# Linear ReLU attention: every octet's Q loaded between K and V, and one octet's Q in five transfers

## The chip, the cores and the metric

The kernel runs on one core of a Trainium2 chip. The metric is the device time of one execution in microseconds (us), taken as the median of several runs of the same program.

## The reference

Q, K and V are 8 x 12 heads of 512 rows of 64 numbers in fp32, the result has the same shape.

```python
Q_feat = np.maximum(0, Q)
K_feat = np.maximum(0, K)
KV = np.einsum('bhkd,bhkv->bhdv', K_feat, V)
K_sum = np.sum(K_feat, axis=2)
numerator = np.einsum('bhqd,bhdv->bhqv', Q_feat, KV)
denominator = np.einsum('bhqd,bhd->bhq', Q_feat, K_sum)
return (numerator / (denominator[:, :, :, None] + 1e-10)).astype(np.float32)
```

Nothing is quadratic in the sequence length: per head there is one 64 x 64 product of K and V, and one product of Q with it.

## The kernel before

The 96 heads are worked on as NO = 12 octets of eight heads. One octet of one tensor is 1 MB of fp32 in DRAM, seen as 128 rows (one for each partition) of 2048 numbers, 8 KB a row. The program moves 36 such blocks in and 12 out.

**Loads.** K and V of octet 0 come by SyncE (SP) in fp32 into two of the output buffers (L267). All else is loaded by GpSimd (POOL) in transfers that cast fp32 to bf16, so that a row of 8 KB arrives as 4 KB: `load_q` (L174) and `load` (L179). There are nine input buffers of each kind (`NI`), so octets 1 to 9 are issued ahead of all work, in program order, and octets 10 and 11 follow the stores of octets 0 and 1. In `load(o)` the order is K, V, Q; for the last octet alone it is K, Q, V (L182 to L187).

**Six lanes.** Each GpSimd transfer signals one of six semaphores in turn (`lane("pool")`, L163). The helper `op` (L58) lists the lane among the things that the transfer writes (L65), so a transfer waits until the one six places before it has landed. Hence six GpSimd transfers at most are in flight, and GpSimd issues the next when the oldest lands.

**One octet's work, `step(i)` (L313).** TensorE transposes Q (L360), multiplies K by V over 64 row blocks into `ps_kv` (L369), transposes the previous octet's result (L378), then computes denominators and numerators (L354). ScalarE applies relu to the transposed Q (`relu_q`, L209), evacuates K-by-V (`evac_kv`, L217), masks a quarter of the next octet's V (`prep_v` as "a0", L200) and copies the numerators out (`copy_ot`, L225). VectorE copies the next octet's Q from its input buffer (`copy_q`, L206), applies relu to the next K (`prep_k`, L191), scales the previous octet's result into an output buffer (`norm`, L242), computes the reciprocals (L230, L234, L237) and masks the rest of the next V (L202). Each engine runs its own list in program order; semaphores tie them together. On ScalarE "a0" stands between `evac_kv` and `copy_ot`, on VectorE `copy_q` stands ahead of `prep_k` and `norm`.

**Stores.** There are seven output buffers (`NOUT`). The stores of octets 0 and 1 are issued by GpSimd among the loads. Those of octets 2 to 11 are issued by SP, and `store` (L246) lists the last octet's K buffer among the things that they read:

```python
keys.append(("k", (NO - 1) % NI))
do.op("sp", lambda e: e.dma_start(out=to, in_=src), reads=keys,
```

So no SP store is issued before K of octet 11 has landed. `norm(9)` writes the buffer that store 2 reads from, and so on: from there a result waits for an older store to land.

## The time and the profile before

| what | value |
|---|---|
| median of 3 runs | 125.52 us (125.49 to 125.57) |
| the profiled execution's own time | 125.56 us |
| its span on the core | 123.7 us |
| TensorE busy | 85.0 us, 69% of the span |
| VectorE busy | 82.4 us, 67% |
| ScalarE busy | 78.3 us, 63% |
| GpSimd busy | 27.6 us, 22%, in 55 instructions |
| read from and written to DRAM | 37.75 MB and 12.58 MB |
| DRAM traffic over the span | 407 GB/s |
| GpSimd transfer of 512 KB (bf16), issue to landing | median 14.4 to 14.5 us |

The span runs from the first to the last recorded event; the profiled time is 1.86 us more. The DMA row of the page is the share of time in which the 16 DMA engines have a packet, averaged over them, in 40 slices of 3.1 us. The GB/s row counts what is written, so a load that casts to bf16 shows half of what it reads.

### The profile page before, as it was taken

The page shows a single profiled execution, that of the slowest core. Times are in us where ns is not written, and L with a number is a line of the kernel's source. Part 1 is how long each engine was busy: PE and PEld are TensorE (multiplying, and loading weights), DVE is VectorE, ACT ScalarE, POOL GpSimd, SP SyncE. Part 2 cuts the span into 40 slices and gives each one's busy share as a digit, 9 for nine tenths or more (in the row PEclk, how much of TensorE's full clock was granted, in tenths as well). Part 3 has the DMA queues.
Part 4 walks back from the last instruction along what each step waited for, and adds up shares of the span by engine and source line. Part 5 has one row for each costly group of instructions (what it writes and reads, how often), then busy time and mean ns, then how long its engine had stood idle before and what let it go on. Part 6 is the DMA issues. An engine that isn't in the chain of part 4 may idle for free.

```text
span 123.7 us, 3402 instructions
## 1 busy us (share of the span) xinstructions
PE 85.0 (69%) x1440; PEld 73.5 (59%) x1440; DVE 82.4 (67%) x127; ACT 78.3 (63%) x108; POOL 27.6 (22%) x55
## 2 busy tenths in 40 slices
PE   0000097697896979969799697996978918983900
PEld 0000096686794867949589485794856916972900
DVE  1261904769789697895987959869688649067330
ACT  0000762998987889878898788987869736652000
POOL 5795311331131213312421142221000000000000
PEclk9999999999999999999999999999999996897555
DMA  3999999999999999999999999999999999999955
GB/s 69 404 315 222 213 215 212 212 212 212 216 215 215 212 212 212 217 215 213 213 215 212 212 212 267 334 215 234 354 217 212 404 424 432 421 421 429 434 238 212
DMA packets 6916, 32.55 MB, mean 263 GB/s; under 512 B 768, under 2 KB 768, under 8 KB 5120
## 3 DMA queue, kind: packets, MB, share of 16 engines
q0 software_dynamic: 5184, 19.93, 75.8%
q1 hardware_dynamic: 1728, 12.58, 24.7%
q14 instruction: 3, 0.02, 0.0%
q8 instruction: 1, 0.02, 0.0%
HBM read 37.75 MB, written 12.58 MB: 407 GB/s over the span
## 4 chain that ended last, share of the span: by engine, by line
DMA 71%; PE 8%; DVE 7%; issue 5%; POOL 4%; POOLq 0%; DVEq 0%; SPq 0%
DMA k_sb<-in_K_dram 54%; DMA q_sb<-in_Q_dram 12%; DMA out_dram<-o_sb 6%; DVE o_sb L242 5%; PE ps_x L378 4%; PE ps_kv L369 2%; POOL vo L263 2%; PE ps_qt L360 1%; DVE ot_sb L225 1%; PE ps_x L354 1%; POOL k_sb L184 1%; POOL mask L263 1%; POOL q_sb L175 1%; POOL v_sb L184 0%; DVE den L234 0%
## 5 line engine op out<-in xcount | busy, mean ns | idle before, releaser
L242 DVE TENSOR_TENSOR o_sb<-ps_x,rec 128x1024 f32<-128x1024 f32 x24 | 28.5, 1217 | 9.2 <-PE ps_x L378 6.6
L225 ACT COPY ot_sb<-ps_x 128x1024 f32<-128x1024 f32 x23 | 23.2, 1013 | 10.7 <-PE ps_x L354 9.8
L369 PE MATMUL ps_kv<-vo,kf 64*128 64x132 bf16 x768 | 26.7, 228 | 0.8 <-DVE vo L202 0.2
L378 PE MATMUL ps_x<-ident,ot_sb 128*128 128x128 f32 x192 | 25.3, 288 | 1.7 <-DVE ot_sb L225 1.7
L369 PEld LDWEIGHTS ps_kv<-vo,kf 64*128 64x128 bf16 x768 | 24.7, 99 | 2.6 <-issue 2.6
L360 PE MATMUL ps_qt<-ident,q 128*128 128x128 bf16 x192 | 14.4, 235 | 16.4 <-DVE q L206 15.4
L209 ACT ACTIVATE qt<-ps_qt 128x1024 bf16<-128x1024 bf16 x24 | 23.4, 1031 | 1.9 <-PE ps_qt L360 1.9
L378 PEld LDWEIGHTS ps_x<-ident,ot_sb 128*128 128x128 f32 x192 | 22.3, 148 | 3.2 <-issue 2.0
L360 PEld LDWEIGHTS ps_qt<-ident,q 128*128 128x128 bf16 x192 | 12.4, 106 | 19.0 <-DVE q L206 15.4
L217 ACT CAST kvd<-ps_kv 64x260 bf16<-64x260 f32 x48 | 17.9, 374 | 8.5 <-PE ps_kv L369 7.6
L354 PE MATMUL ps_x<-qt,kvd 128*128 128x256 bf16 x96 | 14.9, 281 | 12.1 <-DVE o_sb L242 12.0
L191 DVE TENSOR_SCALAR kf<-k_sb,mask 128x2048 bf16<-128x2048 bf16 x22 | 15.6, 750 | 8.5 <-PE ps_kv L369 8.4
L354 PEld LDWEIGHTS ps_x<-qt,kvd 128*128 128x128 bf16 x96 | 7.7, 100 | 16.9 <-DVE o_sb L242 16.3
L206 DVE COPY q<-q_sb 128x2048 bf16<-128x2048 bf16 x12 | 8.2, 686 | 8.6 <-DMA q_sb<-in_Q_dram 8.6
L175 POOL DMA_DIRECT2D q_sb<-in_Q_dram x12 | 9.2, 763 | 19.0 <-DMA q_sb<-in_Q_dram 14.6
L200 ACT ACTIVATE vo<-v_sb,mask 128x1024 bf16<-128x1024 bf16 x11 | 12.7, 1153 | 0.6 <-DMA v_sb<-in_V_dram 0.4
L202 DVE TENSOR_SCALAR vo<-v_sb,mask 128x2048 bf16<-128x2048 bf16 (+1 forms) x22 | 11.6, 568 | 0.0
L184 POOL DMA_DIRECT2D k_sb<-in_K_dram x11 | 7.7, 697 | 16.8 <-DMA k_sb<-in_K_dram 12.9
L184 POOL DMA_DIRECT2D v_sb<-in_V_dram x11 | 6.3, 576 | 16.5 <-DMA v_sb<-in_V_dram 12.7
L200 ACT ACT_TABLE_LOAD x1 | 1.3, 1283 | 12.2 <-DMA o_sb<-in_V_dram 12.2
L354 PE MATMUL ps_kv<-kvd,qt 128*128 128x16 bf16 x192 | 6.9, 179 | 1.7 <-ACT kvd L217 1.7
L354 PEld LDWEIGHTS ps_kv<-kvd,qt 128*128 128x128 bf16 x192 | 6.4, 96 | 2.0 <-ACT kvd L217 1.9
(21 smaller groups left out, 27.6 us busy)
## 6 DMA issues: line engine op xcount, KB each, us to landing
out_dram<-o_sb SPq DMA_DIRECT2D x10, 1024.0 KB, 12.4
q_sb<-in_Q_dram POOLq DMA_DIRECT2D x12, 512.0 KB, 14.5
k_sb<-in_K_dram POOLq DMA_DIRECT2D x11, 512.0 KB, 14.4
v_sb<-in_V_dram POOLq DMA_DIRECT2D x11, 512.0 KB, 14.4
out_dram<-o_sb POOLq DMA_DIRECT2D x2, 1024.0 KB, 14.7
o_sb<-in_K_dram SPq DMA_DIRECT2D x1, 1024.0 KB, 6.2
o_sb<-in_V_dram SPq DMA_DIRECT2D x1, 1024.0 KB, 10.7
```

What stands on the lines that cost most here:

```text
L184: do.op("pool", lambda e: e.dma_start(out=t[i], in_=X[o], single_packet=True), writes=[(n.lower(), i)], dma=lane("pool"))
L191: do.op("dve", lambda e: e.tensor_scalar(kf[:, :, s, :], src, scalar1=0.0, scalar2=mask[:, 0, s:s + 1], op0=Alu.max, op1=Alu.mult), reads= ...
L200: make = lambda e: e.activation(to, src, Act.Copy, scale=m)
L202: make = lambda e: e.tensor_scalar(to, src, scalar1=m, scalar2=None, op0=Alu.mult)
L209: do.op("act", lambda e: e.activation(qt[:, j * (U // 2):(j + 1) * (U // 2)], ps_qt[j], Act.Relu), reads=[("pq", j)], writes=[("qt", j)])
L217: do.op("act", lambda e: e.copy(kvd[64 * c:64 * c + 64, s:8:2, c * D1:c * D1 + D1].rearrange("p (g t) d -> p g t d", t=2), ps_kv[64 * s:64 ...
L225: do.op(who, lambda e: e.copy(to, src) if who == "act" else e.tensor_copy(to, src), reads=[("x", j)], writes=[("ot", j)], sem=f"t{j}")
L242: do.op("dve", lambda e: e.tensor_tensor(o_sb[i][:, rs], ps_x[j].rearrange("p (r d) -> p r d", d=D), rec[:, rs].unsqueeze(2).to_broadcast( ...
L354: return pe.matmul(out_, lhsT, rhs, start=True, stop=True, skip_group_check=True)
L360: x = pe.transpose(ps_qt[u // 8][:, u % 8, :], q2[:, u, :], ident)
L369: x = pe.matmul(ps_kv[:, h, 0:2 * (D + 2)].rearrange("p (t d) -> p t d", t=2), kf[ps, R * g + k, :, :].rearrange("p s d -> p (s d)"), vo[p ...
L378: x = pe.transpose(ps_x[u // 8][:, u % 8 * P:u % 8 * P + P], ot[:, u].rearrange("p h c -> p (h c)"), ident32)
```

## The change

Three things change in the program. `load` puts Q between K and V for every octet, as it was for the last one alone. Q of octet 6, the seventh, is issued as five transfers of 40, 11, 45, 7 and 25 rows, back to back by GpSimd; all five signal one semaphore of their own, "arc", and take no lane, so that V of octet 6 takes the lane that this Q had. Consumers wait for all five (80 counts). The Q buffers are declared flat, which leaves `copy_q` the same 2048 numbers in each partition.

```diff
+    ARCS_AT = 6
+    ARCS = (40, 11, 45, 7, 25)
...
-    def op(self, who, make, reads=(), writes=(), sem=None, dma=None, kept=False):
+    def op(self, who, make, reads=(), writes=(), sem=None, dma=None, kept=False, more=False):
...
-        if kept:
+        if kept or more:
             made.then_inc(self.sems[dma], 16)
             self.count[dma] = self.count.get(dma, 0) + 16
...
     def load_q(o):
-        do.op("pool", lambda e: e.dma_start(out=q_sb[o % NI].rearrange("p u f -> p (u f)"), in_=Qr[o],
-                                            single_packet=True),
+        if o == ARCS_AT:
+            p = 0
+            for n in ARCS:
+                rows = slice(p, p + n)
+                p += n
+                do.op("pool", lambda e: e.dma_start(out=q_sb[o % NI][rows], in_=Qr[o][rows], single_packet=True),
+                      writes=[("q", o % NI)], dma="arc", more=p < P)
+            return
+        do.op("pool", lambda e: e.dma_start(out=q_sb[o % NI], in_=Qr[o], single_packet=True),
               writes=[("q", o % NI)], dma=lane("pool"))
 
     def load(o):
         i = o % NI
         for n, X, t in (("K", Kr, k_sb), ("V", Vr, v_sb)):
-            if n == "V" and o == NO - 1:
+            if n == "V":
                 load_q(o)
             do.op("pool", lambda e: e.dma_start(out=t[i], in_=X[o], single_packet=True), writes=[(n.lower(), i)],
                   dma=lane("pool"))
-        if o < NO - 1:
-            load_q(o)
```

More of the change, by code (lines that the diff above doesn't have):

```diff
@@ L148 @@
     rec = sb.tile([P, RQ], fp32, name="rec")
-    q_sb = [sb.tile([P, U, P], bf16, name=f"q_sb{i}") for i in range(NI)]
+    q_sb = [sb.tile([P, RQ * D], bf16, name=f"q_sb{i}") for i in range(NI)]
     k_sb = [sb.tile([P, RQ * D], bf16, name=f"k_sb{i}") for i in range(NI)]
@@ L158 @@
     names = ["dve", "act", "pool", "pe", "q2", "a0", "d0", "d1", "ev", "t0", "t1", "n0", "n1"]
-    lanes = {"pool": [f"gl{i}" for i in range(LANES)], "sp": [f"sl{i}" for i in range(3)], "last": ["el"]}
+    lanes = {"pool": [f"gl{i}" for i in range(LANES)], "sp": [f"sl{i}" for i in range(3)], "last": ["el"],
+             "arc": ["arc"]}
     sems = {n: tc.alloc_semaphore("s_" + n) for n in names + sum(lanes.values(), [])}
@@ L205, in copy_q @@
     def copy_q(o):
-        do.op("dve", lambda e: e.tensor_copy(q2, q_sb[o % NI]), reads=[("q", o % NI)], writes=["q2"], sem="q2")
+        do.op("dve", lambda e: e.tensor_copy(q2.rearrange("p u f -> p (u f)"), q_sb[o % NI]), reads=[("q", o % NI)],
+              writes=["q2"], sem="q2")
     def relu_q(j):
@@ L287, in body @@
             step(o)
-        for n in lanes["pool"] + lanes["sp"]:
+        for n in lanes["pool"] + lanes["arc"] + lanes["sp"]:
             nc.gpsimd.wait_ge(sems[n], do.count[n])
```

## The prediction, made before the changed kernel ran

> **What bounds the kernel now.** I read the page's slices and its DMA queues first.

> ```profile
> DMA  3999999999999999999999999999999999999955
> ...
> q0 software_dynamic: 5184, 19.93, 75.8%
> q1 hardware_dynamic: 1728, 12.58, 24.7%
> q14 instruction: 3, 0.02, 0.0%
> q8 instruction: 1, 0.02, 0.0%
> ```

> The DMA engines are never idle between the second slice and the last two; no compute engine is above 69%. The 5184 GpSimd packets are 36 transfers x 16 engines x (8 rows + 1 completion). Besides data, four instruction packets share the engines. Next, GpSimd's timeline gives the price of a transfer.

> ```profile
> 36.62 0.53 POOL L184 DMA_DIRECT2D k_sb<-in_K_dram  x1 [1.80 <-DMA k_sb<-in_K_dram]
> 39.08 0.53 POOL L184 DMA_DIRECT2D v_sb<-in_V_dram  x1 [1.93 <-DMA v_sb<-in_V_dram]
> 41.59 0.62 POOL L175 DMA_DIRECT2D q_sb<-in_Q_dram  x1 [1.98 <-DMA q_sb<-in_Q_dram]
> ```

> Each issue waits for the transfer six back. K of octet 3 is issued at 14.54 us and K of octet 9 at 58.74, 18 transfers later: (58.74 - 14.54) / 18 = 2.456 us per 1 MB, so 2.456 / 8 = 0.307 us per row on each engine. Then the chain that ended last, near its end:

> ```profile
> 78.40 14.85 DMA k_sb<-in_K_dram
> 93.25 0.02 issue
> 93.27 7.43 DMA out_dram<-o_sb
> 100.70 0.02 issue
> 100.72 2.37 DVE o_sb L242 x2
> ...
> 117.68 1.23 DVE o_sb L242
> ```

> K of octet 11 lands at 93.25, which lets SP issue store 2; store 2 lands at 100.70, which frees the buffer for `norm(9)`; from there 23.0 us of work follow. VectorE's timeline shows how tight that is:

> ```profile
> 97.19 1.42 DVE L191 TENSOR_SCALAR kf<-k_sb,mask 128x2048 bf16<-128x2048 bf16 x2 [0.72 <-PE ps_kv L369]
> 100.72 2.35 DVE L242 TENSOR_TENSOR o_sb<-ps_x,rec 128x1024 f32<-128x1024 f32 x2 [2.11 <-DMA out_dram<-o_sb]
> ```

> VectorE sat 2.11 us for the store: this is the slack up to which an earlier landing brings the end forward one for one.

> A transfer lands when the last of its 16 engines has finished, and the trace records all 16 completions. In us from the span's start, sorted by time (not by engine number, which it doesn't give):

> ```
> transfer        1st   12th   13th   14th   15th   16th
> K, octet 2    20.16  20.39  20.45  20.53  20.56  21.64
> K, octet 11   91.48  91.83  92.01  92.12  92.16  93.25
> store 2       98.84  99.20  99.49  99.53  99.67 100.70
> store 5      106.21 106.58 106.84 106.91 107.36 108.02
> store 10     118.46 119.02 119.10 119.15 120.18 120.32
> store 11     122.57 122.70 122.72 122.73 122.74 122.75
> ```

> One engine is about 1.1 us behind the next from the start, and every wait for a transfer is a wait for it. The packet records show why: the one "q8 instruction" packet, 16 KB, starts at 4.77 us and takes 0.94 us on one engine, whose own packet beside it takes 0.81 instead of 0.31. Nothing gives the time back, since all engines then do equal work at equal speed. A second engine falls behind late (15th column, 0.1 us ahead of the 16th at store 10), after an instruction packet at 107.21 and a row of its packets at 0.35 to 0.40 us. So the bound is one engine's queue, and at the very end two engines'.

> **The change, part by part.**

> *Q ahead of V.* V of an octet now lands where Q did, one transfer later than its own former place. Its first user is ScalarE's "a0". Octet 2: Q had landed by 26.60 us, "a0" starts at 29.01; these are the rows:

> ```profile
> 26.60 0.69 DVE L206 COPY q<-q_sb 128x2048 bf16<-128x2048 bf16 x1 [1.12 <-DMA q_sb<-in_Q_dram]
> ```

> ```profile
> 29.01 1.15 ACT L200 ACTIVATE vo<-v_sb,mask 128x1024 bf16<-128x1024 bf16 x1
> ```

> That leaves 2.4 us; octets 3, 4, 5 and 10 by the same rows 2.6, 2.9, 2.9 and 2.2. If this cover went, "a0" would hold `copy_ot` behind it on ScalarE, and TensorE's L378. Q comes 2.46 us earlier, which ends VectorE's waits for it (8.6 us in 7); but the next gates, the 0.37 us of `norm(8)` for store 1 and the 2.11 us of `norm(9)` for store 2, are DMA landings. Cost and gain 0 at the end; below zero only if the waits for stores vanished, which they don't.

> *Four more issues.* An issue on GpSimd takes 0.53 to 1.52 us, so five take 2.6 to 7.6 us, from about 37.2 to 39.8 or 44.8. Behind them V of octet 6 waits, and every later load, but six transfers in flight are 6 x 2.456 = 14.7 us of work, to about 51. Cost 0. Without that cover it would be the delay past Q's old slot at 41.59, up to 3.2 us.

> *Four more completions on each engine.* Their records take 0.009 to 0.022 us, while a row follows the one before the completion after 0.306 + 0.006. 4 x 0.006 to 4 x 0.022 = 0.02 to 0.09 us; I take 0.03, by the spacing.

> The five smaller transfers themselves: the queue is full, and the nearest row is the 2.456 us spacing, 427 GB/s. [...]

> *The dealing of rows.* The trace only shows 128 rows dealt 8 to an engine. Of other counts it shows nothing: an engine may get none or several times 8, which moves its queue by -8 x 0.307 = -2.46 us or by more than that upwards. [...] The light places gain 3 x 0.307 = 0.92 and 2 x 0.307 = 0.61 us, the heavy ones lose 0.31. [...]

> *Sum.* If the light places are the two late engines: K 11 lands at 93.25 - 0.92 + 0.03 = 92.36, or, if the next engine is a heavy one, at 92.16 + 0.31 + 0.03 = 92.50. Store 2: 99.81, or 99.67 + 0.34 = 100.01. Gain at `norm(9)` 0.69 to 0.89, well inside 2.11. All later work moves along. At the end store 11 must not queue behind store 10. By the packet records it starts at 119.77 on the first engine and at 119.95 on the late one, which is busy until then; the second late one is free at 119.68. Now these two are free at 119.95 - 0.89 = 119.06 and 119.68 - 0.58 = 119.10, and store 11's issue allows 119.77 - 0.69 to 0.89 = 118.9 to 119.1: the last start moves from 119.95 to about 119.1. Net 0.8 (0.65 to 0.9). The span becomes 123.7 - 0.8 = 122.9, with the 1.86 us around it 124.76; the median is 0.04 below the profiled run: 124.72.

> **The rivals.**

> *The deal misses the late engines.* If the late engine gets 8 rows, only the completions remain: 125.52 + 0.03 = 125.55. If it gets 9, everything after K 11 moves by 0.31 + 0.03: 125.86, slower. For: nothing in the trace numbers the engines. Against: the light places take 0.92 and 0.61 where the profile shows 0.94 lost to one packet and a second engine 1.0 behind the third; with the deal turned, no quantity fits anything.

> *Slower: shares rounded up.* Each piece is dealt in shares of rows / 16 rounded up, from the first engine: 3, 1, 3, 1 and 2. Engines 0 to 6 get 10 rows, 7 to 10 get 9, the last one 0. If the late engine is among the first seven it lags 2 x 0.307 more, K 11 and the end move by 0.61: 126.13 (125.9 for the next four). It decides as soon as the late engine gets 9 rows or more. [...]

> *V becomes the gate.* It needs VectorE's gain from early Q to exceed the 2.2 us of slack; at most 1.23 us of waiting for Q (octet 10) is freed at a time. Then "a0" costs what exceeds it, 0 to 0.3 us: 125.8. The row of 2.2 speaks against.

> *The change does less than it says:* only the late engine is relieved, the second not. Store 11 then can't start on the second engine before 119.68 + 0.03, where the late one stood at 119.95: 0.24 of gain is left, 125.28.

> **How the numbers follow.** A measurement of this kernel can tell about 0.2%, 0.25 us. Forecast 0.60, 124.72, its own range 124.5 to 125.0. Late engine at 8 rows, or only one of two relieved: 0.13, 125.3 to 125.55. Late engine at 9: 0.10, 125.86. Rounded-up shares: 0.12, 126.1. V or another unseen cost: 0.05. Faster 0.60, same 0.13, slower 0.27. The range from 124.5 to 125.9 leaves out the last two.

> **What would show it.** In the changed trace: VectorE's waits for Q gone and no wait of ScalarE for V beyond octet 1; packets of octet 6's Q unequal over the engines; the 16th completion about 0.2 us behind the 15th from octet 6 on instead of 1.1; K 11 at 92.4, store 2 at 99.9, the last `norm` at 116.9. It is wrong if the 16th column keeps its lag or grows, or if `norm(9)` waits for anything but store 2.

## The result: slower by 0.35%

The changed kernel takes 125.91 us (median of 9 runs, 125.83 to 126.47) against 125.49 us for the kernel before in the same session (9 runs, 125.35 to 125.74). The ratio is 1.0035, 95% interval 1.0021 to 1.0048. The prediction was 124.72, with 124.5 to 125.9 as its range.

The profiled execution of the changed kernel took 125.91 us, with a span of 124.1. On its page, the slices and the GpSimd queue:

```profile
DMA  3999999999999999999999999999999999999964
...
DMA packets 7012, 32.55 MB, mean 262 GB/s; under 512 B 864, under 2 KB 864, under 8 KB 5216
...
q0 software_dynamic: 5280, 19.93, 75.7%
```

The engines are as full as before and move the same bytes. There are 96 more small packets (5280 - 5184): 64 are the completions of four more transfers, four for each engine. What the other 32 are follows from the deal below.

GpSimd's timeline around the five pieces shows that issuing them is short:

```profile
37.09 2.52 POOL L185 DMA_DIRECT2D q_sb<-in_Q_dram  x5
39.61 0.55 POOL L196 DMA_DIRECT2D v_sb<-in_V_dram  x1
```

Five issues take 2.52 us, the lower end of what was allowed, and V of octet 6 follows at once. Among the waits, VectorE's 8.6 us for Q are down to one of 0.5; ScalarE's for V is 0.7 in all:

```profile
ACT vo L210 <- DMA v_sb<-in_V_dram: 0.7, 1, 0.7
DVE q L216 <- DMA q_sb<-in_Q_dram: 0.5, 1, 0.5
```

None of that reaches the end. The chain that ended last has the same gates as before:

```profile
93.17 0.02 issue
93.19 7.44 DMA out_dram<-o_sb
100.63 0.02 issue
100.66 2.37 DVE o_sb L253 x2
...
117.93 1.22 DVE o_sb L253
```

K of octet 11 lands at 93.17 (93.25 before) and store 2 at 100.63 (100.70): the expected gain of 0.7 to 0.9 isn't there. VectorE still sits 2.09 us for store 2 ahead of the `norm` of octet 9:

```profile
97.15 1.42 DVE L201 TENSOR_SCALAR kf<-k_sb,mask 128x2048 bf16<-128x2048 bf16 x2 [0.68 <-PE ps_kv L380]
100.66 2.36 DVE L253 TENSOR_TENSOR o_sb<-ps_x,rec 128x1024 f32<-128x1024 f32 x2 [2.09 <-DMA out_dram<-o_sb]
```

The completions of single transfers tell what happened. K and V of octet 6, ahead of and behind the five pieces, sorted by time:

```
K: 49.67 49.72 49.73 49.74 49.76 49.85 49.87 49.89 49.94 49.97 50.03 50.04 50.05 50.06 50.10 | 51.08
V: 52.55 53.34 53.51 54.43 54.77 54.95 55.02 55.18 55.44 55.54 55.57 55.63 55.65 55.91 56.16 | 56.37
```

Fifteen engines that stood within 0.43 us of each other are spread over 3.6 us. V alone is 2.46 us on each engine; what is left of each step is Q's rows at 0.307. With no row an engine gets from about 50.0 to 52.5, with 3 to 53.4, with 4 to 53.7, with 7 to 54.6, with 8 to 54.9, with 9 to 55.2, with 10 to 55.5, and the row of V shows just these steps: one engine at 0, one at 3, one at 4, one at 7, and the rest at 8 to 10. These are the shares of the rival "shares rounded up": 40 rows go 3 at a time to engines 0 to 12 and the last to 13, and so on, each piece from the first engine. The trace doesn't number the engines: an engine's number here and below is its place in this deal. The 32 small packets that were left over fit too. Rounded-up shares of the five pieces leave 8 + 5 + 3 + 9 + 7 = 32 places for a row empty, as if each were filled with a packet of 4 bytes: GpSimd's queue has 672 packets of that size in the trace, against 576 before, which is 64 and 32 more.

The late engine's two transfers take 56.37 - 51.08 = 5.29 us; before, the same stretch took 4.88. It got a ninth row instead of losing three.

At the end, store 10 is complete on its last engine at 120.69 (120.32 before), and store 11, which every engine must queue, at 123.11 (122.75): 2.42 us later in the one, 2.43 in the other. The last `norm` ends 0.24 us later as well, at 119.15 (118.91); the table at the end of the experiments separates the two.

### The profile page after: what moved, and what is told of

Its sections match the earlier page's. It is cut to its first block, busy times and chain, and to the rows that moved or that the text cites. A ratio compares the mean times of both kernels' runs of the same rounds, so it can differ in the third digit from the quotient of the medians.

```text
span 124.1 us, 3407 instructions
## 1 busy us (share of the span) xinstructions
PE 85.8 (69%) x1440; PEld 74.1 (60%) x1440; DVE 82.3 (66%) x127; ACT 78.5 (63%) x108; POOL 28.5 (23%) x59
## 3 DMA queue, kind: packets, MB, share of 16 engines
q0 software_dynamic: 5280, 19.93, 75.7%
q1 hardware_dynamic: 1728, 12.58, 24.8%
HBM read 37.75 MB, written 12.58 MB: 406 GB/s over the span
## 4 chain that ended last, share of the span: by engine, by line
DMA 73%; PE 8%; DVE 7%; issue 4%; POOL 4%; POOLq 0%; DVEq 0%; SPq 0%
DMA k_sb<-in_K_dram 41%; DMA q_sb<-in_Q_dram 14%; DMA v_sb<-in_V_dram 12%; DMA out_dram<-o_sb 6%; DVE o_sb L253 5%; PE ps_x L389 4%; PE ps_kv L380 2%; POOL vo L274 2%; PE ps_qt L371 1%; POOL q_sb L188 1%; DVE ot_sb L236 1%; POOL mask L274 1%; PE ps_x L365 0%; DVE den L245 0%; DVE rec L248 0%
## 5 line engine op out<-in xcount | busy, mean ns | idle before, releaser
L371 PE MATMUL ps_qt<-ident,q 128*128 128x128 bf16 x192 | 15.1, 241 | 16.5 <-DVE q L216 15.4
L371 PEld LDWEIGHTS ps_qt<-ident,q 128*128 128x128 bf16 x192 | 12.9, 109 | 19.3 <-DVE q L216 15.4
L196 POOL DMA_DIRECT2D v_sb<-in_V_dram x11 | 7.6, 694 | 19.4 <-DMA v_sb<-in_V_dram 12.1
L188 POOL DMA_DIRECT2D q_sb<-in_Q_dram x11 | 6.3, 574 | 15.3 <-DMA q_sb<-in_Q_dram 7.0
```

Of the source, the lines that this page charges most:

```text
L196: do.op("pool", lambda e: e.dma_start(out=t[i], in_=X[o], single_packet=True), writes=[(n.lower(), i)], dma=lane("pool"))
L371: x = pe.transpose(ps_qt[u // 8][:, u % 8, :], q2[:, u, :], ident)
```

## The experiments

All are timed against the kernel before on the same chip, except where said. A ratio is taken from the runs beside each kernel, so it can differ a little from the quotient of two medians. Theory A: the ninth row on the late engine delays everything. B: the new order costs. C: five transfers cost by themselves. The later ones add A2: a second late engine, with two rows more, holds the last store; and D: unequal engines cost as such.

**The order alone.**

```diff
-    ARCS_AT = 6
+    ARCS_AT = -1
```

> Q between K and V for every octet, Q of octet 6 in one piece on a lane. Theory A (the ninth row that the five pieces put on the late engine delays everything): 125.5, as before. Theory B (the new order costs): 125.9. Theory C (five transfers cost by themselves: completions, issues, no lane): 125.5.

Measured: 125.60 us, ratio 1.0009 (0.9994 to 1.0025): no difference that can be told, and B's 125.9 (1.0030) lies outside. B falls. Store 2 lands at 100.32 in its profile.

**The pieces alone**, with the order K, V, Q of before.

```diff
-            if n == "V":
+            if n == "V" and o == NO - 1:
                 load_q(o)
...
+        if o < NO - 1:
+            load_q(o)
```

> K, V, Q as before, but octet 6's Q in the five pieces 40, 11, 45, 7, 25. A: 125.85 to 125.9. B: 125.5. C: 125.9.

Measured: 125.83 us, 1.0022 (1.0007 to 1.0037). The pieces carry the loss, as both A and C had it. Store 2 lands at 100.69, 0.37 after that of the order alone.

**Five pieces dealt evenly.**

```diff
-    ARCS = (40, 11, 45, 7, 25)
+    ARCS = (32, 16, 32, 16, 32)
```

> The changed kernel with pieces of 32, 16, 32, 16, 32 rows: still five transfers and 80 completions, but 8 rows for each engine under any deal. A: 125.5 to 125.6 (0.02 to 0.09 for the four more completions). B: 125.9. C: 125.9.

Measured: 125.71 us, 1.0002 (0.9982 to 1.0022). The median is in between, but against the runs beside it there is no loss that can be told: what five transfers, their issues and their completions cost by themselves (C) is at most 0.2%. That alone doesn't clear them, since the pieces alone lost 0.22%. The two later deals in five pieces do, at 1.0001 and 0.9994 with intervals that end at 1.0018 and 1.0009, below the changed kernel's 1.0021. One thing speaks against A already. In this profile K of octet 11 lands at 93.21 and store 2 at 100.62, as late as in the changed kernel and without a ninth row: K of octet 6, ahead of the pieces, was late (51.54, after a step of 2.67).

**A staircase**, to see the deal and to number the late engine.

```diff
-    ARCS = (40, 11, 45, 7, 25)
+    ARCS = (8, 9, 10, 96, 5)
```

> The changed kernel with pieces of 8, 9, 10, 96 and 5 rows. Under rounded-up shares dealt from the first engine, engines 0 to 4 get 10 rows, 5 to 7 get 9, engine 8 gets 8, engine 9 gets 7, engines 10 to 15 get 6. A, with the late engine at 9 rows under 40, 11, 45, 7, 25, so one of engines 7 to 10: its two transfers K-to-V of octet 6 (5.29 us in the changed kernel, 4.88 before) take 5.29 if it is engine 7, 4.98 if 8, 4.67 if 9, 4.37 if 10, and the time is about 125.9, 125.6, 125.3 or 125.0 to 125.1. B and C: 125.9 whatever the counts.

K and V of octet 6 in its profile:

```
K: 49.89 49.92 49.93 49.95 49.96 49.96 49.98 49.98 50.03 50.04 50.05 50.05 50.08 50.09 50.10 | 51.20
V: 54.27 54.32 54.36 54.39 54.39 54.61 | 54.85 | 55.27 55.32 55.33 | 55.50 55.51 55.55 55.58 55.64 | 56.07
```

Six engines at 6 rows, one at 7, three at 9, five at 10, as rounded-up shares say. The one place that is left is 8 rows, and the late engine's step, 56.07 - 51.20 = 4.87, fits it: the late engine is number 8. But the time didn't come out as A had it: 126.03 us, 1.0024 (1.0011 to 1.0038), not 125.6. The late engine had no row more, store 2 landed at 100.34, early, and the last `norm` was early too. The loss is after that, as the end of the chain and SyncE's wait for the last store show, first this kernel's:

```profile
117.14 1.23 DVE o_sb L253
```

```profile
SPq L416 <- DMA out_dram<-o_sb: 4.0, 1, 4.0
```

and then the changed kernel's:

```profile
SPq L416 <- DMA out_dram<-o_sb: 3.1, 1, 3.1
```

`norm` ends at 118.37, 0.8 before the changed kernel's, yet SyncE waits 0.9 longer. Store 10 was complete at 119.95 on fifteen engines and at 120.81 on one, and store 11 came 2.43 later, at 123.24. A second engine sets the end. Kernels with eight rows on both late engines end store 10 at 120.09 to 120.32, so 120.81 is 0.49 to 0.72 later: nearer to two rows more (0.61) than to one (0.31). So it is one of 0 to 4. C, which had 125.9 whatever the counts, isn't ruled out by this time; the next counts do that.

**The kernel before, once more**, because its first profile had a step of 2.84 instead of 2.44 on the late engine at 88.33.

> The kernel before, profiled once more. In its first profile the late engine lost 0.40 us between 85.48 and 88.33 (step 2.84 instead of 2.44), which no other profile has. Theory A (ninth row on the late engine): that loss belongs to one execution, K of octet 11 now lands at about 92.9, as with the order alone, and the changed kernel's 93.17 is 0.3 later. If it lands at 93.25 again, the changed kernel does not lose at that gate.

It gave a single execution of 126.71 us, 1.2 above this kernel's median. The step of 2.84 isn't in it (2.47 and 2.49 at that place), but the late engine lost as much elsewhere: a step of 3.02 at 78.98. K of octet 11 landed at 93.73, not at 92.9. So it isn't shown that the changed kernel loses at that gate: K of octet 11 lands at 93.25 and 93.73 in the kernel before, and at 93.17 in the changed one. What the ninth row does there shows only in the time from K of octet 6 to K of octet 11. It is 42.09 us in the changed kernel and in the pieces alone, 41.67 to 41.85 in four kernels with eight rows on engine 8 (order alone, even pieces and both staircases), and 42.12 and 42.30 in the two profiles of the kernel before, each with one such loss.

**A low staircase**, to number the second engine.

```diff
-    ARCS = (40, 11, 45, 7, 25)
+    ARCS = (1, 2, 3, 4, 118)
```

> Pieces of 1, 2, 3, 4 and 118 rows. Rounded-up shares give 12, 11, 10, 9 rows to engines 0 to 3, 8 to engines 4 to 13, 6 and 0 to the last two; the late engine (number 8 by the stair before) keeps 8. Theory A2 (the end is set by a second late engine, one of 0 to 4, on which the last store queues behind store 10): store 10 lands at 120.2 + 0.31 for each row over 8 on that engine, so the time is 125.5 if it is engine 4, 125.8 if 3, 126.1 if 2, 126.4 if 1, 126.7 if 0. Theory D (unequal engines cost as such, by the spread of 12 rows): 126.1 or more, and no engine stands out at store 10. Theory A alone (only the late engine counts): 125.5.

Measured: 125.47 us, 1.0001 (0.9985 to 1.0018). The piece of one row was not dealt to one engine: the trace has 16 packets of 256 B in its place. So engines 0 to 3 got 11, 11, 10 and 9 rows, not 12, 11, 10 and 9. With up to three rows more they cost nothing, so the second late engine isn't among them: with the staircase before, it is engine 4. (5 to 7, with a ninth row there, would by estimate have shown 0.31, one row's price, about half of what was seen.) D falls: the engines are spread over 11 rows, against 10 in the changed kernel. Here `norm` ends at 117.12, and SyncE waits 4.6 us: TensorE's granted clock was 1.00 from 108 to 119 us (0.84 in the changed kernel), and it brought nothing.

```profile
114.76 2.35 DVE o_sb L253 x2
```

```profile
SPq L416 <- DMA out_dram<-o_sb: 4.6, 1, 4.6
```

**Engines 8 to 15 relieved**, with 16 rows of one Q left out.

```diff
-    ARCS = (40, 11, 45, 7, 25)
+    ARCS = (32, 32, 32, 8, 8)
...
+        memset("dve", q_sb[ARCS_AT][96:P], 0.0, ("q", ARCS_AT))
         prep_k(0, 0)
```

> Pieces of 32, 32, 32, 8 and 8 rows; the last 16 rows of octet 6's Q are left out (zeros from VectorE at the start): engines 0 to 7 get 8 rows, 8 to 15 get 6. A2: the gate at the norm of octet 9 comes 0.61 us earlier than with even pieces, but the second late engine keeps its 8 rows and holds the last store: 0.25 less than even pieces, about 125.3. A alone: 0.6 less, 124.95. D: 125.6 to 125.7.

Measured: 125.32 us, 0.9986 (0.9972 to 1.0000), the 125.3 of A2 rather than the 124.95 of A.

**All engines relieved**, with 32 rows left out: the same memset, and

```diff
-    ARCS = (40, 11, 45, 7, 25)
+    ARCS = (32, 16, 16, 16, 16)
```

> Pieces of 32, 16, 16, 16 and 16 rows; the last 32 rows of octet 6's Q are left out: 6 rows for every engine. A2: both late engines are relieved by 0.61 us, everything from there on moves: 0.6 less than even pieces, 124.95 to 125.05. A alone: the same. D: the same. If it stays at 125.5, the end is not set by the DMA engines at all.

Measured: 125.01 us, 0.9955 (0.9941 to 0.9969), as expected. A, A2 and D all had this; here the time followed the DMA engines' load: 0.48 us less (125.49 to 125.01) with two rows less on each engine.

**The pieces twice**, for octets 4 and 6.

```diff
-    ARCS_AT = 6
+    ARCS_AT = (4, 6)
...
-        if o == ARCS_AT:
+        if o in ARCS_AT:
+            one = f"arc{o}"
```

> The changed kernel's five pieces for Q of octet 4 as well (semaphores of their own): everything that they cost comes twice. A2: engine 4 has 4 rows more than before, 1.23 us, engine 8 has 2 more, 0.61; store 10 ends at about 121.4 on engine 4, and the time is 126.6 to 126.8. If only the late engine counted (A): 126.2. If the cost were the swap or the clock (B): 125.9.

Measured: 126.49 us, 1.0081 (1.0058 to 1.0103): 0.96 above the 125.53 beside it, where the single dose costs 0.42. Only A2 was near, though 0.1 too high: the cost grew with the rows on engine 4, from 0.42 us with two more there (one on engine 8) to 0.96 with four (two on engine 8). Store 10 ends at 121.07, store 11 at 123.49.

**Two deals that leave nothing out**, built for what is now known.

```diff
-    ARCS = (40, 11, 45, 7, 25)
+    ARCS = (112, 4, 4, 4, 4)
```

> Octet 6's Q in pieces of 112, 4, 4, 4 and 4 rows, nothing left out: by rounded-up shares engines 0 to 3 get 11 rows, 4 to 15 get 7. If the late engines are 8 and 4 (theory A2 as the two stairs place them), both lose 0.31 us of work, store 10 ends 0.3 earlier than in the kernel before (the four heavy engines, 0.92 more, stay below: 119.15 + 0.92 = 120.07), and the time is 125.2, below both kernels. If the second late engine is one of 0 to 3: 126.3 to 126.4. D (uneven counts cost as such): above 125.5.

Measured: 125.43 us, 0.9994 (0.9980 to 1.0009); 125.2 was expected. Store 10's last six engines are within 0.66 us, 119.58 to 120.24, as many as the four heavy ones and the two late ones together. Probably heavy ones have taken the late ones' place; I had put them at 120.07 at most, and why they are later isn't shown.

```diff
-    ARCS = (40, 11, 45, 7, 25)
+    ARCS = (112, 4, 4, 8)
```

> Pieces of 112, 4, 4 and 8 rows: engines 0 to 3 get 10 rows, 4 to 7 get 8, 8 to 15 get 7. Engine 8 loses 0.31 us, engine 4 keeps its work. A2: the last store is then held by engine 4 alone, 125.25 to 125.4. If the second late engine is one of 0 to 3: 126.0 to 126.1. D: above 125.5.

Measured: 125.40 us, 0.9985 (0.9971 to 0.9999). It beats both kernels, the one before by 0.15%, about what can just be told. In no deal here did an engine get fewer rows than one with a higher number (10 on the first and none on the last in the changed kernel); where that holds, no deal of all 128 rows lightens engine 4 without loading one of 0 to 3.

**The predicted relief**, three rows off engine 8 and two off engine 4, with 32 rows left out (the memset as above):

```diff
-    ARCS = (40, 11, 45, 7, 25)
+    ARCS = (48, 32, 8, 4, 4)
```

> The relief that the prediction counted on, without its five heavier engines: pieces of 48, 32, 8, 4 and 4 rows, the last 32 rows of octet 6's Q left out. Engines 0 to 3 get 8 rows, 4 to 7 get 6, 8 to 15 get 5, so engine 8 loses 3 rows (0.92 us) and engine 4 two (0.61). If the prediction's sum was right and only the deal wrong: 0.65 to 0.9 below the kernel before, 124.6 to 124.85. If other limits take over first (the 7 to 8 us of matrix work between the last two norms, or engines 0 to 3): 0.5 below at most, as with 6 rows for every engine, 125.0.

Measured: 124.87 us, 0.9951 (0.9937 to 0.9966): 0.60 below the 125.47 beside it, just short of the 0.65 to 0.9. The interval, 0.43 to 0.79 us below, holds both branches of what was expected, and the kernel can't be told from the one with 6 rows for every engine (0.9955). In its profile store 2 is no longer far behind VectorE's own work:

```profile
99.82 2.35 DVE L253 TENSOR_TENSOR o_sb<-ps_x,rec 128x1024 f32<-128x1024 f32 x2 [0.48 <-DMA out_dram<-o_sb]
```

The last `norm` ends at 116.51, store 10 at 119.42 and store 11 at 121.86: the queue still ends the kernel.

One table holds the whole series, from the profiled executions, with their own times. Store 11 is given on its first and its last engine.

| kernel | last `norm` ends | store 10 on its last engine | store 11 | time |
|---|---|---|---|---|
| the predicted relief | 116.51 | 119.42 | 120.23 to 121.86 | 124.61 |
| 8 to 15 relieved | 118.63 | 120.09 | 122.28 to 122.52 | 125.31 |
| 112, 4, 4, 8 | 117.10 | 120.13 | 120.95 to 122.56 | 125.36 |
| order alone | 118.73 | 120.09 | 122.38 to 122.57 | 125.37 |
| low staircase | 117.12 | 120.16 | 120.90 to 122.62 | 125.42 |
| all relieved | 118.81 | 119.53 | 122.46 to 122.65 | 125.44 |
| 112, 4, 4, 4, 4 | 116.37 | 120.24 | 120.79 to 122.68 | 125.48 |
| before | 118.91 | 120.32 | 122.57 to 122.75 | 125.56 |
| even pieces | 119.10 | 120.24 | 122.76 to 122.93 | 125.73 |
| pieces alone | 118.62 | 120.66 | 122.28 to 123.09 | 125.90 |
| changed | 119.15 | 120.69 | 122.80 to 123.11 | 125.91 |
| staircase | 118.37 | 120.81 | 122.02 to 123.24 | 126.04 |
| twice | 119.42 | 121.07 | 123.07 to 123.49 | 126.30 |

Two things can hold store 11. In four kernels (order alone, all relieved, before, even pieces) its sixteen engines finish within 0.2 us of each other, and the last one 3.83 to 3.84 us after the last `norm`: there the issue behind `norm` decides, or is level with the queue. In the nine others the last engine comes later than that, and 2.41 to 2.46 us after store 10 on its last engine: there the queue decides.

So the changed kernel's single profile has two causes. Its last `norm`, 0.24 us later than before, would by itself put store 11 at about 122.98 (119.15 + 3.83); the queue adds 0.13. The later `norm` isn't the heavy engine's doing, since that of the even pieces ends as late. In pieces alone and in the staircase `norm` ends earlier than before, and the queue alone makes the loss: 0.64 and 1.04 us beyond what `norm` allows.

## Why the prediction was wrong

*What bounds the kernel* held: one engine's queue, and at the very end two. The runs number them, 8 and 4, and show that the second counts for more than I gave it: with 8 rows on engine 8 and 10 on engine 4 (the staircase) the kernel already loses 0.24%, which can't be told from the changed kernel's loss. Why the second one falls behind stays open. I had put it after the instruction packet at 107.21, but in the even pieces the last such packet is at 82.34, and a second engine falls behind all the same (0.47 us behind the next at 109.88, 0.78 at 119.98).

*Q ahead of V* held: no cost or gain at the end that can be told (1.0009, 0.9994 to 1.0025).

*Four more issues* held: 2.52 us, covered. *Completions*: four more on each engine held; the packets of 4 bytes in empty places, 32 in all, weren't foreseen. The late engine's step grew by 0.41, of which one row explains 0.31. The other 0.10 isn't explained: in the staircase, with as many small packets and eight rows, the step is 4.87, no longer than before.

*The dealing of rows* is the step that failed. That three rows and two would be taken off the late engines was my assumption, since no row of the profile showed how such counts are dealt, and no run shows either term of the sum for these pieces. The traces show the rounded-up deal from the first engine for every piece of 2 to 118 rows, and not for that of a single row. So the late engine 8 got 9 rows and engine 4 got 10, against 8 before; the sum's -0.92 and -0.61 are +0.31 and +0.61.

The rival "shares rounded up" was this, down to its price for engines 7 to 10, "125.9 for the next four"; I gave it 0.12, and 126.1 as its middle, since I took the late engine to be among the first seven. What spoke for the forecast, that the light places matched the lags in size, was about the numbers in the change and not about the chip.

*The sum* was nearly right for the relief that it assumed: 0.60 (0.43 to 0.79) measured, with no engine heavier and 32 rows less to move, where 0.65 to 0.9 was said.

One reading was off in the profile of before. Its K of octet 11 at 93.25 contains 0.40 us that the late engine lost at 88.33, so an engine that stays 1.1 us behind is not the whole of it. The other profile of this kernel has a loss of that size at another place, and the even pieces one of 0.2 ahead of the pieces. A single pair of profiles doesn't show a ninth row at this gate: the changed kernel's 93.17 is 0.27 after the order alone, but earlier than the 93.25 that the forecast started from.

## What to carry to other kernels

When a kernel is bound by its DMA queues, look at the completions of single engines: here a transfer landed with its slowest engine (K of octet 11 at 93.25 in the kernel before, with fifteen engines done at 92.16), and a lag made once mostly stayed up to store 10: the changed kernel's engines were 3.82 us apart behind the pieces (52.55 to 56.37) and still 3.07 there (117.62 to 120.69). Before row counts are used to steer work between engines, measure how a transfer of an odd count is dealt; one run with a staircase of sizes shows it. And weigh a forecast by what the trace shows of its least known step, not by how well the numbers in the change would fit.

## What the runs showed of the hardware

Such a transfer has more packets of 4 B than its 16 completions, one for each place that the rounding leaves empty: 32 for the changed kernel's pieces, 16 for 32, 32, 32, 8 and 8 rows, 48 for 112, 4, 4, 4 and 4, none for the even pieces.

A row on one engine took 0.307 us there (2.456 us for eight). The two more on engine 4 in the staircase, dealt at about 55 us, are still 0.5 to 0.7 us at the end of store 10 (120.81 against 120.09 to 120.32).

The end of the compute moved with TensorE's granted clock, in the low staircase without effect on the time (1.00 from 108 to 119 us, ratio 1.0001). From the norms of octet 9 to the end of the last `norm` it was 18.49 us in the changed kernel and 16.70 in the predicted relief. The windows between 104 and 108 us, first of the changed kernel, then of the relief, show the clock beside it; the third number from the right is the clock:

```profile
104.00:108.00 4.00, 4.00 (x72) 3.80 (x71) 1.15 (x3) 2.63 (x3) 0.00 (x0) 0.57 1.01 424
```

```profile
104.00:108.00 4.00, 3.96 (x87) 3.85 (x86) 1.05 (x2) 3.23 (x6) 0.00 (x0) 1.00 1.01 422
```

The clock records put each half-speed stretch that ends before the matrix work does at 3.41 us (102.94 to 106.35 in the kernel before) or at 6.83, twice that (100.51 to 107.34 with all engines relieved). Ahead of 104 us VectorE had waited 0.48 us for store 2 in the relief and 2.09 in the changed kernel; the low staircase ran at 0.81 from 104 to 108 us after a wait of 1.21. No run changed the wait alone, so it isn't shown that the shorter wait kept the clock up.
